# Running sums of the log gates: made once per 512 columns and loaded per chunk, with the chunks' factor differences on GpSimd

## The chip, the cores and the metric

One core of one Trainium2 chip runs the whole step in one launch. Its engines are TensorE (PE, with its weight loads PEld), VectorE (DVE), ScalarE (ACT), GpSimd (POOL) and SyncE (SP), which issues every DMA. The metric is the device time of one execution in microseconds (us), lower is better.

## The reference, cut to what matters

One layer of a hybrid encoder is computed for 2064 prompt rows (16 meta rows and 2048 new ones) and for 8 sample streams of 16 rows. Two mixers run on the same input: gated linear attention (GLA) and sparse attention over selected keys. The change concerns the gates of the first:

```python
log_f = log_sigmoid(g_low @ gla_w2 + gla_gate_b) / 16        # [t, 4 heads, 128]
# per block of tokens, heads apart:
b = cumsum(log_f, axis=tokens)
a[i, j] = sum_d q[i,d] k[j,d] exp(b[i,d] - b[j,d])   for j <= i
o = (q * exp(b)) @ S + a @ v
S = exp(b_end)[:, None] * S + (k * exp(b_end - b)).T @ v
```

## The kernel before, in words

Phase 1 makes all projections in three groups of columns and writes them to HBM (`d_...`). Phase 2 runs the sparse attention for the query blocks 15 down to 8, then blocks 7 to 0 together with the GLA projection, then the merge and the output projection.

*The attention* of a block makes, per head, logits in PSUM (lines 1110 and 1111, tile `pl`, 3 buffers). DVE reads each piece out of PSUM, adds the mask and takes the maximum (line 1112: `lgl`, `lgu`, `mx`). ACT takes the exponential (line 1117), PE transposes the probabilities (line 1046, `px`), ACT or DVE copies them out (1054, 1056), and PE multiplies with the values (1070, `oo`).

*The side work* is a generator (`side_work`, line 1214) that the attention advances as it goes: `gla_gates`, the samples' attention (`attend_sample`), the samples' GLA (`gla_sample`), the meta rows (`gla_meta`), then 16 chunks of 128 tokens (`gla_chunk`). Its first 13 steps are given a priority 1500 ahead, so that they run beside the last projections of phase 1.

*The gates* (`gla_gates`, line 652) go through the 2192 columns in 5 slices of up to 512, each in two groups of two heads: four `[128, 512]` products on PE (line 666, `pg`, 2 buffers), absolute value on ACT (667), minimum on DVE (668, `gx`), exponential and logarithm on ACT, subtraction on POOL (675), and a store of the log gates to `d_lf` (676). The tiles `gx` and `ge` of `[128, 2, 512]` share three buffers.

*A chunk* loads its 128 columns of log gates (683, `x`), and DVE makes the running sums with one scan per head (687, `b`, restarted by the zero in `rst`). `gla_factors` (693) then takes differences of those sums: 12 tensor-tensor instructions on DVE for a chunk and 6 for the samples, into `f`; ACT takes the exponential of `f` (715) and of `x` (859). `gla_pairs` and three `gla_level`s scale q and k with these factors on POOL (`q`, `m`, `mq`), PE multiplies them (735, 756), and DVE puts the blocks into the matrix `a` with masked copies (737, 738, 761). The next chunk's `b` may be written when the exponential of the last sum (864, `end`) has read this chunk's.

The order of each engine's instructions is fixed when the program is built: a scheduler plays the program through on a timeline of its own and writes down, engine by engine, what it would start first, with priorities given by the place in the source. An engine then works through its list strictly in order, so one instruction that waits holds up all behind it. A changed duration or dependency moves rows on every engine from that point on.

Of the kernel before, what the change touches and what calls it, by code (L numbers as in the profile page):

```python
# [10 lines left out]
F32 = mybir.dt.float32  # L11
# [6 lines left out]
OP = mybir.AluOpType  # L18
# [3 lines left out]
P = 128  # L22
DM = 1024
KT = 8
META = 16
# [51 lines left out]
TT = META + NT * P  # L77
# [8 lines left out]
def nkeys(j):  # L86
    return META + P * (j + 1)
# [31 lines left out]
class Trunk:  # L119
# [73 lines left out]
    def scratch(self, ctx):  # L193
        dr = ctx.enter_context(self.tc.tile_pool(name="dr", bufs=1, space=DRAM))
        d = {}
        for n, s, t in (
            ("gq", [512, TT], F32), ("gk", [512, TT], F32), ("gl", [16, TT], F32), ("lf", [512, TT], F32),
            ("gv", [TT, 1024], F32), ("gr", [TT, 1024], F32),
            ("q", [2048, TT], F32R),
            ("ih", [512, TT], F32R), ("il", [512, TT], F32R),  # L200
            ("kd", [P, 4, TT], F32R), ("v", [TT, 256], F32), ("z", [TT, 1024], F32),
            ("ma", [1024, TT], F32), ("mb", [1024, TT], F32),
            ("oa", [1024, TT], F32), ("ob", [1024, TT], F32), ("ya", [1024, TT], F32), ("h", [TT, 1024], F32),
        ):
            d[n] = dr.tile(s, t, name="d_" + n)
        d["mask"] = {j: dr.tile([P, nkeys(j)], BF16, name=f"d_mask{j}") for j in range(16)}
        d["mask"]["s"] = dr.tile([P, SKEY], BF16, name="d_masks")
        d["xt"] = [dr.tile([P, KT, n], F32, name=f"d_xt{q}") for q, n in enumerate(PCN)]
        self.d = d
# [441 lines left out]

    def gla_gates(self):

        nc = self.nc
        for c in range(0, TT, 512):
            n = min(512, TT - c)
            gl = self.gt.tile([16, 512], F32, name="gl", tag="x")
            nc.sync.dma_start(gl[:, :n], self.d["gl"][:, c : c + n])
            xs, es = [], []
            for g in range(2):  # L660
                x = self.sb.tile([P, 2, 512], F32, name="gx", tag="s4", bufs=SKB)
                e = self.sb.tile([P, 2, 512], F32, name="ge", tag="s4", bufs=SKB)
                for u in range(2):
                    h = 2 * g + u
                    ps = self.pg.tile([P, 512], F32, name="pg")
                    nc.tensor.matmul(ps[:, :n], self.w2[:, h * P : (h + 1) * P], gl[:, :n], start=True, stop=True)
                    self.act(e[:, u, :n], ps[:, :n], AF.Abs, bias=self.gb[:, h : h + 1])
                    self.ts(x[:, u, :n], ps[:, :n], self.gb[:, h : h + 1], OP.add, 0.0, OP.min)
                self.act(e[:, :, :n], e[:, :, :n], AF.Exp, scale=-1.0)
                xs.append(x)  # L670
                es.append(e)
            for g in range(2):
                x, e = xs[g][:, :, :n], es[g][:, :, :n]
                self.act(e, e, AF.Ln, bias=1.0)
                self.tt(x, x, e, OP.subtract, eng=nc.gpsimd)
                nc.sync.dma_start(self.d["lf"][2 * g * P : (2 * g + 2) * P, c : c + n].rearrange("(h p) t -> p h t", p=P), x)
            yield

    def gla_decay(self, c, r):

        nc = self.nc
        x = self.gt.tile([P, 4, P], F32, name="x")
        nc.sync.dma_start(x[:, :, :r], self.d["lf"][:, c : c + r].rearrange("(h p) t -> p h t", p=P))
        b = self.gt.tile([P, 4, P + 1], F32, name="b")
        nc.gpsimd.memset(b[:, :, 0:1], 0.0)
        for h in range(4):
            nc.vector.tensor_tensor_scan(b[:, h, 1 : 1 + r], self.rst[:, h, :r], x[:, h, :r], 0.0, OP.mult, OP.add)
        return x, b

    def gla_eng(self, kind):  # L690
# [2 lines left out]
    def gla_factors(self, b, levels):  # L693


        e = self.nc.vector
        f = self.gt.tile([P, 924], F32, name="f")
        out, at = [], 0
        for r, s in levels:
            n = P // (r * s)  # L700
            first = b[:, :, :P].rearrange("p h (n c s) -> p h n c s", c=r, s=s)[:, :, :, :, 0]
            last = b[:, :, 1:].rearrange("p h (n c s) -> p h n c s", c=r, s=s)[:, :, :, :, s - 1]
            group = lambda t, w: t.to_broadcast([P, 4, n, w])
            def put(w, x, y):
                nonlocal at
                t = f[:, at : at + 4 * n * w]
                at += 4 * n * w
                self.tt(t.rearrange("p (h n c) -> p h n c", h=4, n=n), x, y, OP.subtract, eng=e)
                return t.rearrange("p (m c) -> p m c", c=w)
            fs = [put(r, first, group(first[:, :, :, 0:1], r)), put(r, group(last[:, :, :, r - 1 : r], r), last)]  # L710
            if r == 4:
                fs.append(put(2, first[:, :, :, 2:4], group(last[:, :, :, 0:1], 2)))
                fs.append(put(1, first[:, :, :, 3:4], last[:, :, :, 1:2]))
            out.append(fs)
        self.act(f[:, :at], f[:, :at], AF.Exp, scale=1.0 / 16)
        return out
# [754 lines left out]
```

## Time and profile before

| | before |
|---|---|
| median of 3 runs | 3657.09 us (3652.93 to 3662.06) |
| the profiled execution, its own time | 3653.39 us |
| its span, first to last instruction | 3651.6 us |
| busy: PE, DVE, ACT, POOL | 96%, 70%, 40%, 29% |
| mean granted clock of TensorE | 0.985 |

The profile is of one execution. Busy times overlap from engine to engine, and a PE that is shown busy may still be waiting inside a pipelined instruction. In the span the gates' stage lies at 1677 to 1745 us, phase 1's last projection ends at about 1858 us, the samples' GLA runs from about 1914 us, and the 16 chunks from about 2010 to 2690 us.

### The profile page before, as it was taken

The numbers are of one execution on the slowest core, as the hardware profiler recorded it, in microseconds if no ns is written. First come the engines' busy times: TensorE is split into PE (matmuls) and PEld (weight loads), VectorE is DVE, ScalarE is ACT, GpSimd is POOL, SyncE is SP. The second block draws the span as 40 slices with busy tenths as digits, with TensorE's granted clock in tenths as the row PEclk, the third lists the DMA queues.
The fourth block names the chain that finished last, engine by engine and source line by source line (L and its number), as shares of the span: only waits on it lengthen the run. The fifth ranks groups of instructions, "written<-read, shape, count | busy, mean of one in ns | idle before, by whom it ended". The sixth has DMA issues, their size and how long they took to land.

```text
span 3651.6 us, 65899 instructions
## 1 busy us (share of the span) xinstructions
PE 3516.6 (96%) x24196; PEld 3224.6 (88%) x24196; DVE 2568.0 (70%) x5971; ACT 1451.5 (40%) x3084; POOL 1048.6 (29%) x1220
## 2 busy tenths in 40 slices
PE   7999999999999999999989999999999999989999
PEld 7999999999999999998976778777778888879998
DVE  7748997799999988943246877777765666555444
ACT  4444223433334234325434555555665443431110
POOL 3122343242343344344301433334410000012221
PEclk9999999999999999999999999999999999999999
DMA  8642443263442345363653333233343345564432
GB/s 266 196 127 84 136 124 96 84 180 106 122 127 75 117 136 166 115 173 122 160 170 106 84 92 85 80 92 85 85 116 89 94 106 138 150 193 140 121 114 62
DMA packets 535810, 448.78 MB, mean 123 GB/s; under 512 B 94032, under 2 KB 507856, under 8 KB 535488
## 3 DMA queue, kind: packets, MB, share of 16 engines
q1 hardware_dynamic: 535488, 444.58, 42.4%
q8 instruction: 190, 3.11, 0.4%
q14 instruction: 132, 1.08, 0.1%
HBM read 288.01 MB, written 156.44 MB: 122 GB/s over the span
## 4 chain that ended last, share of the span: by engine, by line
PE 75%; DVE 13%; DMA 5%; ACT 2%; issue 2%; POOL 1%; SPq 1%; POOLq 0%; DVEq 0%; ACTq 0%
PE pp L266 12%; PE pp L264 12%; PE pp L265 12%; PE oo L1070 6%; PE px L1046 4%; PE pd L264 3%; PE pd L266 3%; PE pd L265 3%; PE pl L1110 2%; PE pl L1111 2%; PE fo L264 2%; PE fo L265 2%; PE fo L266 2%; DVE junk L149 1%; DVE sc L152 1%
## 5 line engine op out<-in xcount | busy, mean ns | idle before, releaser
L149 DVE TENSOR_SCALAR_CACHE_REDUCE junk<-sc,cand 128x272 bf16<-128x272 f32 (+6 forms) x512 | 701.7, 1371 | 17.0
L143 POOL TENSOR_TENSOR wlo<-raw,whi 128x512 fp32r<-128x512 f32 x360 | 487.9, 1376 | 768.0 <-ACT whi L158 704.3
L266 PE MATMUL pp<-whi,xl 128*128 128x256 f32 (+3 forms) x1952 | 560.4, 288 | 4.4 <-DVE xl L143 4.4
L264 PE MATMUL pp<-whi,xh 128*128 128x256 f32 (+3 forms) x1952 | 561.7, 288 | 3.1 <-ACT whi L158 2.1
L264 PE MATMUL pp<-xh,whi 128*128 128x384 f32 (+2 forms) x1728 | 563.0, 326 | 1.4 <-ACT whi L158 1.4
L265 PE MATMUL pp<-xl,whi 128*128 128x384 f32 (+2 forms) x1728 | 563.2, 326 | 0.0
L266 PE MATMUL pp<-xh,wlo 128*128 128x384 f32 (+2 forms) x1728 | 562.1, 326 | 0.1
L265 PE MATMUL pp<-wlo,xh 128*128 128x256 f32 (+3 forms) x1952 | 560.9, 288 | 0.0
L266 PEld LDWEIGHTS pp<-whi,xl 128*128 128x128 f32 (+1 forms) x1952 | 370.4, 190 | 14.6 <-DVE xl L143 6.9
L264 PEld LDWEIGHTS pp<-whi,xh 128*128 128x128 f32 (+1 forms) x1952 | 371.4, 190 | 11.2 <-issue 3.0
L265 PEld LDWEIGHTS pp<-wlo,xh 128*128 128x128 f32 (+1 forms) x1952 | 371.4, 190 | 5.4 <-issue 2.3
L1112 DVE CUSTOM_DVE_ANT_0 lgl<-pl,mkl 128x348 f32<-128x348 f32 (+8 forms) x608 | 297.3, 510 | 83.6 <-PE pl L1111 48.0
L1110 PE MATMUL pl<-kd,q 128*128 128x348 f32 (+14 forms) x800 | 308.1, 388 | 32.7 <-DVE mx L1112 23.9
L264 PE MATMUL pd<-xh,wh 128*128 128x242 f32 (+3 forms) x1152 | 327.9, 285 | 8.6 <-ACT wh L1328 3.8
L264 PEld LDWEIGHTS pp<-xh,whi 128*128 128x128 f32 x1728 | 324.4, 188 | 2.7 <-ACT whi L158 2.0
L266 PE MATMUL pd<-xh,wl 128*128 128x242 f32 (+3 forms) x1152 | 324.6, 282 | 0.8 <-POOL wl L143 0.8
L265 PE MATMUL pd<-xl,wh 128*128 128x242 f32 (+3 forms) x1152 | 325.1, 282 | 0.3 <-DVE xl L143 0.3
L266 PEld LDWEIGHTS pp<-xh,wlo 128*128 128x128 f32 x1728 | 324.1, 188 | 1.2 <-POOL wlo L143 0.4
L265 PEld LDWEIGHTS pp<-xl,whi 128*128 128x128 f32 x1728 | 324.4, 188 | 0.7
L158 ACT CAST whi<-raw 128x512 fp32r<-128x512 f32 (+1 forms) x344 | 199.1, 622 | 314.8 <-DMA raw<-in_w_in 201.3
L155 ACT ACTIVATE lgl<-lgl,mx 128x1040 f32<-128x1040 f32 (+7 forms) x256 | 249.8, 976 | 181.5 <-DVE mx L1114 177.6
L1118 POOL COPY pmeta<-lgl 128x48 f32<-128x48 f32 x256 | 58.7, 229 | 771.4 <-ACT lgl L155 765.0
(250 smaller groups left out, 7842.7 us busy)
## 6 DMA issues: line engine op xcount, KB each, us to landing
raw<-in_w_in SPq DMA_DIRECT2D x360, 256.0 KB, 3.2
q<-d_q SPq DMA_DIRECT2D x272, 128.0 KB, 3.0
d_h<-x SPq DMA_DIRECT2D x17, 512.0 KB, 3.4
d_gv<-en SPq DMA_DIRECT2D x68, 128.0 KB, 2.1
d_gr<-en SPq DMA_DIRECT2D x68, 128.0 KB, 1.8
d_z<-en SPq DMA_DIRECT2D x68, 128.0 KB, 1.7
gr<-d_gr SPq DMA_DIRECT2D x17, 512.0 KB, 3.6
v<-d_gv SPq DMA_DIRECT2D x17, 512.0 KB, 3.9
```

Source lines behind the costliest of these rows:

```text
L143: (eng or self.nc.vector).tensor_tensor(out, a, b, op=op)
L149: (eng or self.nc.vector).tensor_scalar(out, a, s1, s2, op0=op0, op1=op1, **kw)
L155: self.nc.scalar.activation(out, a, f, **kw)
L158: (self.nc.vector.tensor_copy if self.spare else self.nc.scalar.copy)(out, src)
L264: mm(ps, ah(k), bh(k), start=k == 0, stop=False)
L265: mm(ps, ah(k), bl(k), start=False, stop=False)
L266: mm(ps, al(k), bh(k), start=False, stop=k == n - 1)
L1046: nc.tensor.transpose(ps[:, 2 * s + u, :], pe[u][a // KLOW][:, a % KLOW : a % KLOW + P], self.ident[:])
L1070: self.nc.tensor.matmul(oo[0][64 * o : 64 * o + 64, k : k + 2, :], self.v[:, s0 + s, d : d + 64], t[:, 2 * s : 2 * s + 2], start=self.fres ...
L1110: nc.tensor.matmul(ps[:, :m], q[:, u, :], kd, start=True, stop=False)
L1111: nc.tensor.matmul(ps[:, :m], q[:, 2 + u, :], kd, start=False, stop=True)
L1112: nc.vector.tensor_tensor_reduce(lg[z1][:, a : a + m], ps[:, :m], mk[z1][:, a : a + m], 1.0, NEG, OP.add, OP.max, mx[:, s : s + 1])
```

## The change

- A new scratch array `d_ls` holds running sums. After the subtraction, the gates' stage runs the scan over its whole slice on DVE, two heads of `[128, 400]`, `[128, 512]` or `[128, 256]` per group, into the tile `ge`, and stores it to `d_ls` beside `d_lf`. `rst` is read flat, so the sums restart every 128 columns.
- The slices are cut at chunk boundaries: 400 columns (the 16 meta columns are scanned apart), three times 512, and 256. There are still five.
- A chunk loads its sums into `b` by a second DMA in place of four scans.
- The differences in `gla_factors` go to POOL; the loop, the instructions and their shapes are the same.

```diff
     def gla_gates(self):
-        for c in range(0, TT, 512):
-            n = min(512, TT - c)
+        rst = self.rst[:].rearrange("p c t -> p (c t)")
+        cuts = [0, *range(META + 3 * P, TT, 512), TT]
+        for c, end in zip(cuts, cuts[1:]):
+            n = end - c
...
                 self.act(e, e, AF.Ln, bias=1.0)
                 self.tt(x, x, e, OP.subtract, eng=nc.gpsimd)
-                nc.sync.dma_start(self.d["lf"][2 * g * P : (2 * g + 2) * P, c : c + n].rearrange("(h p) t -> p h t", p=P), x)
+                for a, b in ((0, META), (META, n)) if not c else ((0, n),):
+                    for u in range(2):
+                        nc.vector.tensor_tensor_scan(e[:, u, a:b], rst[:, : b - a], x[:, u, a:b], 0.0, OP.mult, OP.add)
+                for name, t in ("lf", x), ("ls", e):
+                    nc.sync.dma_start(self.d[name][2 * g * P : (2 * g + 2) * P, c : c + n].rearrange("(h p) t -> p h t", p=P), t)
             yield
     def gla_decay(self, c, r):
         x = self.gt.tile([P, 4, P], F32, name="x")
-        nc.sync.dma_start(x[:, :, :r], self.d["lf"][:, c : c + r].rearrange("(h p) t -> p h t", p=P))
         b = self.gt.tile([P, 4, P + 1], F32, name="b")
         nc.gpsimd.memset(b[:, :, 0:1], 0.0)
-        for h in range(4):
-            nc.vector.tensor_tensor_scan(b[:, h, 1 : 1 + r], self.rst[:, h, :r], x[:, h, :r], 0.0, OP.mult, OP.add)
+        for t, src in (x[:, :, :r], "lf"), (b[:, :, 1 : 1 + r], "ls"):
+            nc.sync.dma_start(t, self.d[src][:, c : c + r].rearrange("(h p) t -> p h t", p=P))
         return x, b
     def gla_factors(self, b, levels):
-        e = self.nc.vector
+        e = self.nc.gpsimd
```

Three places show what that does to the order. Line numbers behind the change are six higher (L761 becomes L767, L1112 becomes L1118). First DVE in the middle of the chunks, before: the attention's reads of PSUM are `lgl` and `lgu`, the scans of the next chunk are `b<-rst,x`, printed there as a scalar-tensor-tensor form.

```order
L761 COPY_PREDICATED a<-lm,pg 128x32x6
L687 SCALAR_TENSOR_TENSOR b<-rst,x 128x128 x4
L1112 ISA lgl,mx<-pl,mkl 128x348
L1112 ISA mx 128x1
L1112 ISA lgl,mx<-pl,mkl 128x344
L1112 ISA mx 128x1
L983 RECIPROCAL rs<-sums 128x8
L761 COPY_PREDICATED a<-lm,pg 128x32x6
```

At the like place, the masked copies of a chunk's last level, the changed program has on DVE:

```order
L767 COPY_PREDICATED a<-lm,pg 128x32x6
L1120 TENSOR_REDUCE mx<-mx 128x1
L767 COPY_PREDICATED a<-lm,pg 128x32x6
L767 COPY_PREDICATED a<-lm,pg 128x32x4
L1118 ISA lgl,mx<-pl,mkl 128x348
L1118 ISA mx 128x1
L767 COPY_PREDICATED a<-lm,pg 128x32x4
L1062 COPY st_25770<-px 128x512
```

The four scans ahead of the attention's reads are gone, and so are the runs of 12 differences `f<-b` that stood some 20 rows further on. Those runs now stand on POOL, between a chunk's last products and the next chunk's first; on that engine the changed program has:

```order
L143 TENSOR_TENSOR m<-m,f 128x512
L143 TENSOR_TENSOR mq<-mq,f 128x512
L143 TENSOR_TENSOR f<-b 128x256 x2
L143 TENSOR_TENSOR f<-b 128x128
L143 TENSOR_TENSOR f<-b 128x64 x3
L143 TENSOR_TENSOR f<-b 128x32
L143 TENSOR_TENSOR f<-b 128x16 x3
L143 TENSOR_TENSOR f<-b 128x8
L143 TENSOR_TENSOR f<-b 128x4
L143 TENSOR_TENSOR m<-k,x 128x256
L143 TENSOR_TENSOR mq<-q,x 128x64x4 x2
```

POOL works through one chunk after the other, and the differences are queued in that one line. In the gates' stage DVE of the changed program has the new scans (line 681, `ge<-rst,gx`) among the minima `gx`, the copies of projections `en` and the casts of weights `whi`:

```order
L149 TENSOR_SCALAR gx<-pg,gb 128x512 x2
L158 CAST whi<-raw 128x512 x2
L158 COPY en<-pp 16x256
L158 CAST whi<-raw 128x512
L681 SCALAR_TENSOR_TENSOR ge<-rst,gx 128x512 x2
L158 COPY en<-pp 128x256
L149 TENSOR_SCALAR gx<-pg,gb 128x512 x2
L158 COPY en<-pp 128x256
L681 SCALAR_TENSOR_TENSOR ge<-rst,gx 128x512 x2
L149 TENSOR_SCALAR gx<-pg,gb 128x512 x2
```

Each pair of scans stands ahead of the next group's minima.

## Rows read from the trace of the kernel before

**Rows 1.** The page, part 1: busy time, share of span, instructions per engine.
```profile
PE 3516.6 (96%) x24196; PEld 3224.6 (88%) x24196; DVE 2568.0 (70%) x5971; ACT 1451.5 (40%) x3084; POOL 1048.6 (29%) x1220
```

**Rows 2.** Stages: window, length, each engine busy (instructions), granted clock, DMA share, GB/s.
```profile
2038.00:2639.00 601.00, 565.38 (x3835) 466.67 (x3834) 455.30 (x1632) 338.12 (x724) 231.53 (x364) 0.98 0.31 85
2640.00:2690.00 50.00, 49.24 (x346) 40.72 (x346) 34.17 (x129) 29.57 (x75) 12.40 (x23) 1.00 0.26 69
1677.00:1745.00 68.00, 68.00 (x440) 51.65 (x439) 26.33 (x46) 59.64 (x67) 36.20 (x22) 1.00 0.44 138
1850.00:1900.00 50.00, 39.62 (x196) 31.96 (x196) 25.16 (x91) 20.60 (x45) 1.37 (x5) 0.83 0.68 192
```

**Rows 3.** The same view: 14 stretches of 8 us around the scans.
```profile
2195.00:2203.00 8.00, 6.15 (x32) 5.62 (x31) 7.39 (x25) 4.35 (x8) 3.57 (x7) 0.81 0.48 151
...
2322.00:2330.00 8.00, 5.17 (x27) 4.56 (x26) 7.56 (x27) 4.95 (x10) 4.76 (x7) 0.79 0.28 78
...
sum 112.00, PE 97.31 PEld 79.67 DVE 95.72 ACT 68.14 POOL 60.89; mean PE 6.95 PEld 5.69 DVE 6.84 ACT 4.87 POOL 4.35
```

**Rows 4.** The same view: 15 stretches of 8 us around the differences.
```profile
2163.00:2171.00 8.00, 4.96 (x29) 3.87 (x29) 7.25 (x29) 4.61 (x9) 5.07 (x7) 0.89 0.22 53
...
sum 120.00, PE 103.60 PEld 83.40 DVE 108.62 ACT 66.30 POOL 66.81; mean PE 6.91 PEld 5.56 DVE 7.24 ACT 4.42 POOL 4.45
```

**Rows 5.** Order of time, 2322 to 2328 us: start, length, operation [idle before].
```profile
2322.33 0.50 DVE L1112 CUSTOM_DVE_ANT_0 lgl<-pl,mkl 128x348 f32<-128x348 f32 x1
...
2322.76 3.14 DVE L687 TENSOR_TENSOR_SCAN b<-rst,x 128x128 f32<-128x128 f32 x4
...
2323.23 0.31 PE L1111 MATMUL pl<-kd,q 128*128 128x320 f32 x1
...
2325.82 0.48 DVE L1112 CUSTOM_DVE_ANT_0 lgl<-pl,mkl 128x344 f32<-128x344 f32 x1
...
2326.36 0.66 PE L1110 MATMUL pl<-kd,q 128*128 128x348 f32 x1 [2.83 <-DVE mx L1112]
```

**Rows 6.** Waits, 2038 to 2640 us: total us, times, longest us.
```profile
PEld pl L1110 <- DVE mx L1112: 28.2, 30, 3.1
...
PE pl L1110 <- DVE mx L1112: 20.8, 14, 2.8
...
POOL mq L143 <- ACT f L155: 16.1, 9, 2.7
```

**Rows 7.** Groups of instructions, whole span: count, busy us, mean ns, idle before.
```profile
L756 PE MATMUL pg<-mq,m 128*128 128x192 f32 (+1 forms) x400 | 81.9, 331 | 0.9 <-POOL pmeta L1118 0.5 <-DVE mx L1114 0.2 <-DVE state L152 0.2
...
L143 DVE TENSOR_TENSOR f<-b 128x128 f32<-128x128 f32 (+4 forms) x198 | 55.5, 348 | 2.0 <-POOL mq L143 1.9
...
L687 DVE TENSOR_TENSOR_SCAN b<-rst,x 128x128 f32<-128x128 f32 (+1 forms) x72 | 40.0, 615 | 2.3 <-DMA x<-d_lf 2.3
...
L666 PE MATMUL pg<-gl,w 16*128 16x512 f32 (+1 forms) x40 | 19.4, 573 | 0.0
```

**Rows 8.** Line 687, the scans: shortest, median and longest in ns.
```profile
L687 DVE TENSOR_TENSOR_SCAN b<-rst,x x72: 162/410/1317, 1914.3 to 2616.4; 128x128 f32<-128x128 f32 x68, 128x16 f32<-128x16 f32 x4
```

**Rows 9.** Groups by shape on POOL, 1900 to 2700 us.
```profile
L143 POOL TENSOR_TENSOR mq<-mq,f 128x256 f32<-128x256 f32 x49 | 32.5, 664 | 17.9 <-ACT f L155 17.3
...
L1118 POOL COPY pmeta<-lgl 128x48 f32<-128x48 f32 x102 | 24.0, 235 | 248.5 <-ACT lgl L155 242.1 <-DMA q<-d_q 5.5 <-PE pl L1111 0.7
...
L143 POOL TENSOR_TENSOR mq<-mq,f 128x128 f32<-128x128 f32 x49 | 21.4, 436 | 0.0
L143 POOL TENSOR_TENSOR m<-k,x 128x256 f32<-128x256 f32 x17 | 15.6, 920 | 29.5 <-issue 28.1 <-POOL mq L143 1.4
```

**Rows 10.** Tile gx: shortest, median, longest ns; first and last start; landing.
```profile
L149 DVE TENSOR_SCALAR gx<-pg,gb x20: 357/742/754, 1679.9 to 1740.0; 128x512 f32<-128x512 f32 x16, 128x144 f32<-128x144 f32 x4
...
DMA to landing us min/median/max: 1.9/2.8/3.5
```

**Rows 11.** SP's own waits: total us, times, longest us.
```profile
SPq L683 <- POOL mq L143: 73.4, 14, 12.5
```

More of the change, by code (lines that the diff above doesn't have):

```diff
@@ L196, in scratch @@
         for n, s, t in (
-            ("gq", [512, TT], F32), ("gk", [512, TT], F32), ("gl", [16, TT], F32), ("lf", [512, TT], F32),
+            ("gq", [512, TT], F32), ("gk", [512, TT], F32), ("gl", [16, TT], F32), ("lf", [512, TT], F32), ("ls", [512, TT], F32),
             ("gv", [TT, 1024], F32), ("gr", [TT, 1024], F32),
```

## The prediction

> **What bounds the kernel now.** I read the busy shares first: PE 3516.6 us of a 3651.6 us span, 96% [rows 1]. Work taken from DVE or given to POOL therefore counts only where PE waits for it. The table of stages says where that is. In the chunks' stage, 2038 to 2639 us, PE is busy 565.38 of 601 us, so it idles 35.6 us, with a granted clock of 0.98; right behind the last differences, 2640 to 2690 us, it idles 0.8 of 50 us at 1.00; in the gates' stage, 1677 to 1745 us, it idles not at all [rows 2].
>
> Next I cut the chunks' stage where the changed instructions stand. Fourteen stretches of 8 us around the chunks' scans hold 112 − 97.31 = 14.7 us of PE idle [rows 3], fifteen around the differences 120 − 103.60 = 16.4 us [rows 4]. Together that is 31.1 of the stage's 35.6 us in 232 of its 601 us. The other 369 us have 4.5 us, 1.2%. DVE is busy 95.72 + 108.62 = 204.3 of 232 us there, 88%, and (455.3 − 204.3) / 369 = 68% elsewhere.
>
> One stretch in order of time shows the mechanism. DVE reads a piece of logits, then runs four scans for 3.14 us; the next read starts at 2325.82; PE, which needs the PSUM buffer, stands until 2326.36 and has idled 2.83 us, put down to DVE's maximum [rows 5]. The list of waits agrees: PE and its weight loads wait for that line 20.8 and 28.2 us in this stage (the two overlap and are not added), 2.8 and 3.1 us at the longest [rows 6]. The clock follows: three of the stretches shown have 0.81, 0.79 and 0.89 granted, which means that part of each ran at the lower of the two levels, 1.2 GHz [rows 3, 4].
>
> **Term 1, the bursts leave DVE.** 68 scans of 128 columns and 4 of 16 go (40.0 us with what they are held up), and 198 differences (55.5 us) [rows 7]. Fifteen chunks' differences and fourteen chunks' scans lie in the stretches above, about 55.5 × 15 / 17 + 40.0 × 14 / 18 = 80 us of the 204.3. What is left there is 124 of 232 us, 53%, less than the 68% at which PE lost 1.2%. At that rate the stretches would still idle 2.8 us, so at most 31.1 − 2.8 = 28.3 us of idle can go. The clock costs (1 − 0.98) × 601 = 12 us, 9 to 15 with the rounding; I count half, 6 us, since part of it runs while PE stands idle anyway. The ceiling is 28.3 + 6 = 34 us, or 43 if nothing of the clock's loss overlaps. I take three quarters of 34, 26 us: DVE keeps the masked copies and state updates of the same chunk, and the list is scheduled anew, so some waits will reappear at other rows. The floor is nothing gained, if the waits only move. The samples' and the meta rows' bursts before 2038 us I count at nothing; they come on top if anything.
>
> **Term 2, the differences on POOL.** Per chunk: two of 256 elements, one of 128, three of 64, one of 32, three of 16, one of 8 and one of 4. POOL takes 664 to 920 ns for 256, 436 for 128, and 235 ns for a copy of 48 [rows 9]. With 0.84, 0.44 and, for the nine small ones, 0.28 between the last two, that is 1.7 + 0.4 + 2.5 = 4.6 us a chunk and about 75 us in all; 50 us if all are as quick as that copy, 100 us if the small ones take what 128 does. POOL is busy 231.5 of 601 us, 39%, so it ends near 50% [rows 2]. What hides it is the attention: PE lost 0.9 us in all in front of the 400 products that POOL feeds [rows 7]. The cost is nothing as long as a chunk's chain has that slack; what it costs without it is the slower rival below.
>
> The trace shows that DVE's scans pay for POOL's company: 410 ns at the median and 1317 at the longest for the same instruction [rows 8]. The Trainium skill, "SBUF — State Buffer" (Who interferes with whom), says that a DVE instruction with two SBUF inputs and a GpSimd one that reads SBUF exclude each other for a whole instruction; "Perfetto Trace Analysis" (Optimizing Scalar/DVE Operations) warns that moving work between the two might therefore not help. Here it speaks less against the move than it seems: the scans and differences are the two-input instructions, and both leave this stage's DVE, while the reads of PSUM run at 0.48 to 0.50 us right beside POOL's work [rows 5]. By the warning term 1 would be nothing, which is the second case below.
>
> **Term 3, the gates' stage.** Added on DVE are 24 scans: twelve of 512 columns, four each of 384, 256 and 16. From 162 ns (16 columns) to 410 (128) is 2.2 ns a column [rows 8], so 1.26, 0.98 and 0.69 us for the long ones, 22 us in all. Held up by POOL each adds up to 1317 − 410 = 0.9 us, 44 us in all. DVE is busy 26.3 of 68 us there, ACT 59.6 [rows 2]: ACT sets the pace, 60.1 us for nine steps of a group, 6.7 us each [rows 10]. A pair of scans is 2.5 to 4.3 us and stands ahead of the next group's minima (0.74 us each), which free the PSUM buffers for line 666. That line waits for nothing now [rows 7], and the changed list puts more projection rows between its products. I take 3 us: that a pair of scans delays a weight cast or a minimum once or twice. Bounds: nothing, if ACT stays the slower; 12 us, if all scans slow down in proportion (1317 / 410 = 3.2, so 4.0 us each and 8 us a pair, 1.3 us over a step of 6.7 us, nine times).
>
> **Term 4, DMAs and the change of phase.** Ten stores and 18 loads are added on SP. A chunk's `b` must wait for the previous chunk's last exponential; behind that wait on SP stand loads of q for the attention. SP already waits 73.4 us for the slot of `x`, once 12.5 us [rows 11], in a stage where PE idles 35.6 us in all, so the loads of q bear waits of that kind. The gates' longer chain also pushes the samples' work later, from beside the last projections into the change of phase, where PE idles 10.4 of 50 us at 0.83 [rows 2]. It can fill that hole or lengthen the chain behind it: −4 to +6 us, taken as +1.
>
> **Sum.** −26 + 0 + 3 + 1 = −22 us against the profiled execution's 3653.39, 3631. The median of the runs lies 3.7 us above that execution, so 3635 us.
>
> **Rivals.**
> - The waits only move (no change, 3655 us). DVE's bursts go, but the masked copies, POOL's later products and the new order take their place, and term 1 returns a quarter or less: −6 + 4 = −2 us. For it: every list from the gates on is new, and DVE stays about 60% busy. Against it: 87% of the idle lies in 39% of the stage, exactly at these instructions.
> - POOL becomes the chunk's bound (slower, 3670 us). POOL does one chunk after another, and the differences now stand between the last product of one and the first product of the next, where DVE made them beside POOL's work. POOL already waits 16.1 us for the exponential of these factors [rows 6], so they are on the chunk's chain. It decides once a chunk's first product comes later than PE's list has it by more than the slack: then PE stands, in order, with the attention behind it. Fully exposed that is 15 × 4.6 = 69 us; half exposed, as I take it, 35 us, and with −26 of term 1 and +4 of terms 3 and 4 that is +13 us on 3657. Against it: 0.9 us lost there now, and POOL half idle.
> - The whole ceiling comes (3618 us): −43 + 4 = −39 us from 3657.
>
> **Chances.** Forecast (3635) 0.50, ceiling 0.12, no change 0.23, POOL 0.15. What a measurement of this kernel can tell from no change is 0.3%, 11 us, so faster means under 3646. The forecast falls short of that in a few cases of its own, which the no-change case gives back in part: faster 0.61, same 0.24, slower 0.15. The range takes in the ceiling and reaches to where the POOL case begins: 3608 to 3668 us; the forecast's own is 3622 to 3646.
>
> **What would show it.** In the changed profile the chunks' stage should hold about 12 us of PE idle in place of 35.6, with a clock of 0.99 or more; PE's waits at the logits for DVE's maximum should fall to half; DVE's total should fall by some 60 us and POOL's rise by 50 to 100. Term 2 is wrong if PE's idle in front of the level products (now 0.9 us) grows to several us or POOL's differences average over 0.6 us; term 3 if PE idles in the gates' stage; term 4 if the hole at the change of phase grows. The forecast as a whole fails if the chunks' stage is not shorter.

## The result: 3602 us, faster, by more than the range allowed

| | before | changed |
|---|---|---|
| median | 3657.32 us (3652.93 to 3662.06, 4 runs) | 3602.16 us (3595.52 to 3604.86, 4 runs) |
| span of the profiled execution | 3651.6 us | 3598.6 us |
| mean granted clock | 0.985 | 0.99 |

The ratio is 0.9846, with a 95% interval of 0.9827 to 0.9865. The direction was forecast, the size was not: 22 us were forecast, 55 came, and the range ended at 3608 us.

The page's part 1 of the changed kernel, to be read against [rows 1]:

```profile
PE 3487.7 (97%) x24196; PEld 3215.9 (89%) x24196; DVE 2512.2 (70%) x5725; ACT 1450.1 (40%) x3084; POOL 1107.5 (31%) x1418
```

DVE lost 56 us and 246 instructions, POOL gained 59 us and 198. PE has the same number of matmuls as before and is still busy 29 us less. The stages, as in [rows 2] (the chunks' stage, the stretch behind it, the gates' stage, the change of phase, each where it now lies):

```profile
2060.00:2637.00 577.00, 568.62 (x3997) 481.23 (x3994) 404.00 (x1458) 346.98 (x760) 289.69 (x561) 1.00 0.36 99
2637.00:2690.00 53.00, 44.92 (x309) 34.26 (x308) 32.52 (x114) 36.56 (x80) 10.35 (x17) 0.94 0.54 151
1682.00:1762.00 80.00, 78.00 (x493) 61.34 (x494) 47.95 (x69) 59.42 (x66) 38.19 (x22) 0.96 0.52 173
1860.00:1910.00 50.00, 43.67 (x255) 35.70 (x255) 32.10 (x118) 26.48 (x57) 1.40 (x6) 0.90 0.78 214
```

In the chunks' stage PE idles 8.4 us in place of 35.6, at a clock of 1.00 in place of 0.98. But look at the matmuls: 3997 in 577 us, 142.3 ns of busy time each, where before there were 3835 in 601 us, 147.4 ns each. For 3835 matmuls the stage now needs 554 us, 47 less. Idle is 27.5 us of that, and 20 us come out of time that was shown as busy. The mix of matmuls differs between the two windows, so this split is rough.

To compare equal work I cut the trace at matmuls: from the first product of the attention's logits (line 1110, now 1116) to its 576th, the last of blocks 15 to 8. The same table for that stretch, of the kernel before:

```profile
1870.00:2803.00 933.00, 877.34 (x5883) 710.17 (x5883) 672.72 (x2381) 516.38 (x1103) 289.23 (x471) 0.97 0.34 93
```

and of the changed one:

```profile
1874.50:2754.40 879.90, 853.97 (x5911) 706.07 (x5911) 598.55 (x2130) 516.93 (x1110) 342.53 (x668) 0.99 0.38 106
```

Nearly the whole gain lies here: 53 us, of which 30 are idle (55.7 to 25.9 us) and 23 busy time. The clock is a large part of the second: by the trace's records of it 50 us of the stretch were at the lower level before and 16.5 are now. At half speed that is 25 and 8 us of clock not granted, 17 us less. The stretch begins 4.7 us later than before (1869.8 to 1874.5), and what follows it is 4.7 us shorter (848.9 to 844.2).

The waits at the logits over 680 us (2010 to 2690; total, times, longest), of the kernel before:

```profile
PEld pl L1110 <- DVE mx L1112: 29.8, 34, 3.1
...
PE pl L1110 <- DVE mx L1112: 21.2, 16, 2.8
```

and of the changed one:

```profile
PEld pl L1116 <- DVE mx L1118: 5.0, 13, 1.0
...
PE pl L1116 <- DVE mx L1118: 1.6, 4, 0.7
```

Waits of 3 us are gone; what is left is at most 1.0 us. One chunk's start in order of time, which answers to [rows 5]:

```profile
2242.22 3.67 POOL L143 TENSOR_TENSOR f<-b 128x256 f32<-128x256 f32 x12
...
2242.55 0.51 DVE L1118 CUSTOM_DVE_ANT_0 lgl<-pl,mkl 128x344 f32<-128x344 f32 x1
...
2243.24 0.42 PE L1116 MATMUL pl<-kd,q 128*128 128x384 f32 x1
2243.25 0.55 DVE L1118 CUSTOM_DVE_ANT_0 lgu<-pl,mku 128x384 f32<-128x384 f32 x1
...
2243.92 0.55 DVE L1118 CUSTOM_DVE_ANT_0 lgu<-pl,mku 128x384 f32<-128x384 f32 x1
2244.19 0.46 PE L1116 MATMUL pl<-kd,q 128*128 128x348 f32 x1
```

POOL makes all twelve differences in 3.67 us while DVE reads logits at 0.51 to 0.55 us a piece, and no product of PE shows an idle time ahead of it.

Groups of instructions, whole span, to be read against [rows 7 and 10]:

```profile
L762 PE MATMUL pg<-mq,m 128*128 128x192 f32 (+1 forms) x400 | 80.6, 329 | 2.4 <-POOL mq L143 2.2
...
L143 POOL TENSOR_TENSOR f<-b 128x128 f32<-128x128 f32 (+4 forms) x198 | 61.8, 353 | 5.7 <-DMA b<-d_ls 4.7
...
L681 DVE TENSOR_TENSOR_SCAN ge<-rst,gx 128x512 f32<-128x512 f32 (+3 forms) x24 | 28.0, 1214 | 18.7 <-POOL gx L143 18.7
...
L669 PE MATMUL pg<-gl,w 16*128 16x512 f32 (+2 forms) x40 | 19.7, 576 | 1.5 <-DVE gx L149 1.5
```

The differences cost POOL 61.8 us, 353 ns each, and 4.7 us of waiting for the loaded sums. PE waits 2.2 us in all for POOL's products. The gates' scans take 28.0 us. SP's wait for the slot of `x` fell from 73.4 us [rows 11] to 42.7:

```profile
SPq L693 <- POOL mq L143: 42.7, 13, 8.8
```

### The profile page after: what moved, and what is told of

Its sections match the earlier page's. It is cut to its first block, busy times and chain, and to the rows that moved or that the text cites. A ratio compares the mean times of both kernels' runs of the same rounds, so it can differ in the third digit from the quotient of the medians.

```text
span 3598.6 us, 65922 instructions
## 1 busy us (share of the span) xinstructions
PE 3487.7 (97%) x24196; PEld 3215.9 (89%) x24196; DVE 2512.2 (70%) x5725; ACT 1450.1 (40%) x3084; POOL 1107.5 (31%) x1418
## 5 line engine op out<-in xcount | busy, mean ns | idle before, releaser
L1118 DVE CUSTOM_DVE_ANT_0 lgl<-pl,mkl 128x348 f32<-128x348 f32 (+8 forms) x608 | 296.4, 511 | 103.3 <-PE pl L1117 65.2
L152 DVE SCALAR_TENSOR_TENSOR sc<-rl,iw,sc 128x388 f32<-128x388 f32 (+16 forms) x308 | 216.9, 743 | 71.4 <-ACT rl L155 70.0
```

The costliest lines, as they stand in the source:

```text
L152: self.nc.vector.scalar_tensor_tensor(out, a, s, b, op0=op0, op1=op1)
L1118: nc.vector.tensor_tensor_reduce(lg[z1][:, a : a + m], ps[:, :m], mk[z1][:, a : a + m], 1.0, NEG, OP.add, OP.max, mx[:, s : s + 1])
```

## Experiments

Theory A is the prediction's mechanism: the chunks' scans and differences hold up DVE's reads of logits, and what leaves DVE comes back as time of PE. Rivals: what got shorter is the chunk's own chain of work, whose sums are now loaded ahead, and DVE's time as such does not matter (B); the two parts relieve DVE only together (C); and, after the first four runs, O: a good part of the gain is only another order of the rows, which any change of a duration brings. Each run was timed beside the kernel before, whose medians were 3652 to 3656 us in these sets; a ratio is to that, with its 95% interval.

**The parts alone.** Sums made with the gates and loaded, differences left on DVE (diff against the changed kernel):

```diff
-        e = self.nc.gpsimd
+        e = self.nc.vector
```

> Scans in the gates' stage and loaded by chunks, differences left on DVE. Theory A (what DVE has in its list beside the attention's reads costs, each burst for itself): the scans' stretches held a bit under half of PE's idle and more than half of the low clock, less some 5 us in the gates' stage: about 25 us faster than before, 3632 us (3622 to 3642). Rival B (the chunk's chain is what got shorter, since its sums are loaded ahead and nothing on DVE precedes them; DVE's time as such does not matter): nearly the whole gain, 3600 to 3612 us. Rival C (the two parts relieve DVE only together, below some load): at most 10 us faster, 3647 to 3657 us.

Measured: 3616.63 us, 0.9903 (0.9874 to 0.9932).

Only the differences moved (gates' stage, stores and chunk scans as before, `e = self.nc.gpsimd`):

> Differences on GpSimd, scans left where they were. A: about 30 us faster than before, 3627 us (3617 to 3637), so that with the scans' part the 55 us are made up. B: no gain, 3650 to 3660 us, since the chain keeps its scans and gets slower differences. C: at most 10 us faster, 3647 to 3657 us.

Measured: 3632.78 us, 0.9946 (0.993 to 0.9961). Each part has a gain alone, 36 and 20 us, which add up to the 55, where B expected none of the differences and C at most 10 us of either. The sums gave more than A allows them (3622 us at the least). Taken by themselves these two runs do not part A from O, since the next ones show that another order alone is worth 20 us.

The gates' stage as changed, with sums made and stored that nobody loads; the chunks work as before (diff against the changed kernel):

```diff
-        for t, src in (x[:, :, :r], "lf"), (b[:, :, 1 : 1 + r], "ls"):
-            nc.sync.dma_start(t, self.d[src][:, c : c + r].rearrange("(h p) t -> p h t", p=P))
+        nc.sync.dma_start(x[:, :, :r], self.d["lf"][:, c : c + r].rearrange("(h p) t -> p h t", p=P))
+        for h in range(4):
+            nc.vector.tensor_tensor_scan(b[:, h, 1 : 1 + r], self.rst[:, h, :r], x[:, h, :r], 0.0, OP.mult, OP.add)
...
-        e = self.nc.gpsimd
+        e = self.nc.vector
```

> The gates' stage makes and stores the sums as in the changed kernel, but nobody loads them: a chunk makes its own with scans, and the differences stay on DVE. It prices what is added in the gates' stage alone. A and C: 3 to 9 us slower than before, 3660 to 3666 us, at the end of phase 1. B: the same price. Another reading, that the new order of the rows alone brought the gain: faster than before by 10 us or more.

Measured: 3632.38 us, 0.994 (0.9919 to 0.9962). This kernel only adds work, takes nothing from the chunks, and is 20 us faster. A, B and C had it 3 to 9 us slower; the other reading named there, that the new order alone brings a gain, is the one that came. No cost of an instruction explains it, and it is where theory O comes from.

Four unread scans in each chunk of the changed kernel, first form:

```diff
+        w = self.gt.tile([P, 4, P], F32, name="w")
+        for h in range(4):
+            nc.vector.tensor_tensor_scan(w[:, h, :r], self.rst[:, h, :r], x[:, h, :r], 0.0, OP.mult, OP.add)
```

> The changed kernel, and each chunk also runs four scans of its log gates on DVE into a tile that nobody reads, so DVE has the scans' time back while no chain depends on them. A: it loses what the scans' part gained, 25 to 30 us, and comes to 3625 to 3635 us. B: within 5 us of the changed kernel, 3597 to 3607 us. C: most of the gain goes, 3640 us or more.

Measured: 3680.7 us, 1.0075 (1.0051 to 1.0099). It is not the test that was meant: all but 4 of the gates' 40 products came after the last projection of phase 1 (1813 us), the last of them at 1906 us in place of 1756. The new tile lies in the chunks' pool, and I take it that it moved other tiles, which the trace does not show. The run says nothing of the scans.

**The order alone.** One number of the scheduler's priorities, no work added or removed, first in the kernel before and then in the changed one:

```diff
-EARLY = 1500
+EARLY = 1400
```

> The kernel before with one number of the planner changed (EARLY 1500 to 1400): no work is added or removed on any engine; from the last projection of phase 1 on the rows come in another order, and the samples' part ends later among the attention's work, as it does in the changed kernel. Theory A (the gain of the changed kernel is VectorE's relief from the chunks' bursts): 3645 to 3662 us, no change. Theory O (about 20 us of the 55 are the order of the rows, as the run that only made the sums in the gates' stage suggests): 3625 to 3642 us, and fewer stretches of the attention at a clock below 1.00. Any value outside 3620 to 3665 says that the order alone moves more than either theory gives it.

Measured: 3625.01 us, 0.9925 (0.991 to 0.994): 29 us faster with the same instructions. Its waits at the logits over the same 680 us:

```profile
PEld pl L1110 <- DVE mx L1112: 21.4, 30, 3.5
PE pl L1110 <- DVE mx L1112: 14.0, 12, 3.1
```

They are about as long as before, one by one, but there are fewer. The time is in O's range; A had expected no change.

> The changed kernel with the same number changed (EARLY 1500 to 1400), the work on every engine as in the changed kernel. Theory A: 3595 to 3610 us, as the changed kernel. Theory O: the order's share may be lost or not, 3595 to 3625 us; above 3615 it would say that a good part of the gain hangs on one order of the rows.

Measured: 3609.81 us, 0.9884 (0.9869 to 0.9899), which both theories allow.

The kernel before with the new cuts of the gates' slices alone:

```diff
-        for c in range(0, TT, 512):
-            n = min(512, TT - c)
+        cuts = [0, *range(META + 3 * P, TT, 512), TT]
+        for c, end in zip(cuts, cuts[1:]):
+            n = end - c
```

> The kernel before with the changed kernel's cuts of the gates' stage alone (400, 512, 512, 512 and 112 columns at the end in place of 512 steps from 0); scans and differences stay in the chunks on VectorE. Theory A: no change, 3645 to 3662 us. Theory O: as the run that only made the sums, 3625 to 3640 us, since that run differs from before in the cuts, the sums and the order that follows from them. If it is as slow as before, the cuts are not what gave that run its 20 us.

Measured: 3633.72 us, 0.9948 (0.9933 to 0.9963), as fast as with the unread sums, and again in O's range and not in A's. (The last slice has 256 columns, not the 112 that the expectation names.) So the sums themselves cost the gates' stage nothing that shows: the first product of the logits starts at 1874.3 us with the cuts alone, at 1874.5 in the changed kernel.

Two more orders of the kernel before (EARLY 1450 and 1600) and one of the changed kernel (1600):

> The kernel before with EARLY 1450, no work added or removed: a third order of the rows; the chunks' part lies between those of 1500 (the kernel before) and 1400. Reading U (the order of the kernel before is an unlucky one, by some 20 us): 3620 to 3640 us. Reading L (the order at 1400 is a lucky one): 3645 to 3660 us.

> The kernel before with EARLY 1600: a fourth order, in which the samples' part and the chunks begin earlier among the attention's work than in any of the others. Reading U: 3620 to 3642 us. Reading L: 3645 to 3665 us. If the place of the side work among the attention is what counts (later is better), this is the slowest of all, 3655 to 3675 us.

> The changed kernel with EARLY 1600: work on every engine as in the changed kernel, but samples and chunks begin as early among the attention's work as in the kernel before. If the relief of VectorE is worth 25 to 32 us whatever the order, and that place costs 20: 3615 to 3630 us. If the place costs only where VectorE has the bursts (order and relief are one and the same gain): 3598 to 3610 us. Above 3635 the change would have no gain of its own in this order.

Measured: 3642.34 us, 0.9965 (0.9953 to 0.9977); 3649.56 us, 0.998 (0.9968 to 0.9991); 3605.56 us, 0.9861 (0.9844 to 0.9877). Neither "unlucky" nor "lucky" is the whole story, and the changed kernel at 1600 came out where relief and order are one gain (3598 to 3610), not where the relief is worth 25 to 32 us whatever the order (3615 to 3630). By EARLY:

| | 1400 | 1450 | 1500 | 1600 | cuts only |
|---|---|---|---|---|---|
| before | 3625.0 | 3642.3 | 3657.3 | 3649.6 | 3633.7 |
| changed | 3609.8 | | 3602.2 | 3605.6 | |

The same work takes 32 us more or less in the kernel before, and 8 in the changed one. Every order of the changed kernel is faster than every order of the kernel before; the gain is 15, 55 or 44 us at equal EARLY. The kernel before stands at the slow end of its orders, the changed kernel at the fast end of its own. Place does not decide it: 1600 brings the side work earliest and is slow with the bursts, not without them. Nor do the waits at the logits rank the orders: at 1600 they are 14.2 us on PEld and 7.3 on PE, less than the 21.4 and 14.0 at 1400, in a kernel that takes 25 us longer. What makes one order of the kernel before slower than another stays open.

Some of these kernels can be compared with less of the order in it. In seven of them the stretch from the logits' first product to the 576th holds the very same 5912 matmuls, by what they write and read, and in the first two of these in the very same order. In the mean a matmul of the other six stands 6 to 20 places from where it stands in the changed kernel's stretch. Their lengths (the last three kernels come in the next part):

| | stretch, us | PE idle | DVE busy |
|---|---|---|---|
| before, EARLY 1400 | 911.5 | 44.7 | 666.1 |
| sums made, unread (the gates' stage as changed) | 911.2 | 46.6 | 667.5 |
| sums made and loaded, differences on DVE | 897.2 | 36.1 | 635.1 |
| changed: differences on POOL too | 879.9 | 25.9 | 598.6 |
| changed, four unread scans in a row | 904.5 | 43.4 | 629.7 |
| changed, unread scans spread, first form | 910.0 | 43.2 | 625.3 |
| changed, unread scans spread, second form | 890.2 | 32.0 | 630.9 |

With the gates' stage kept as changed, loading the sums shortens the stretch by 14 us and moving the differences by another 17; the whole times, 3632, 3617 and 3602 us, fall by 16 and 14. The second step leaves the chunk's chain its links and only takes the differences off DVE (353 ns each on POOL, 348 on DVE before), so B does not explain it. The orders still differ a little from step to step, and the changed kernel's orders by EARLY differ by 8 us.

**The load put back.** Four unread scans per chunk again, in a pool of their own, meant to move no other tile; PE's order stays close to the changed kernel's:

```diff
+        if r == P and self.spares:
+            w = self.spares.tile([P, 4, P], F32, name="w")
+            for h in range(4):
+                nc.vector.tensor_tensor_scan(w[:, h, :r], self.rst[:, h, :r], x[:, h, :r], 0.0, OP.mult, OP.add)
...
+            self.spares = inner.enter_context(tc.tile_pool(name="spares", bufs=1, side="right"))
```

> The changed kernel with four scans on VectorE in every 128-row chunk whose result nobody reads, in a pool of its own so that the other tiles stay where they are; the order of TensorE's rows is the changed kernel's for the phases up to the last sixth. It adds 64 scans or so of about 0.6 us, 35 to 40 us on VectorE, as the chunks of the kernel before had them. Theory A: what the scans cost in place comes back, 16 us as the step from the sums alone to sums loaded by the chunks gave: 3612 to 3625 us, and the clock dips behind the bursts return. Theory O: the order is kept, so no more than 5 us: 3598 to 3607 us.

Measured: 3621.89 us, 0.9915 (0.9898 to 0.9931), 20 us slower than the changed kernel, as A has it and O has not. The long waits are back; in order of time PE's idle stands right behind the scans, though these took only 1.36 us here. The dips of the clock that were expected hardly came back: by the trace's records of the clock 10 of these 680 us are at the lower level, where the kernel before has 31 and the changed one 7. Waits over the 680 us:

```profile
PEld pl L1120 <- DVE mx L1122: 16.0, 25, 4.2
PE pl L1120 <- DVE mx L1122: 9.7, 10, 3.8
```

Order of time:

```profile
2311.14 2.34 DVE L149 TENSOR_SCALAR ss<-ss 128x2 f32<-128x2 f32 x1 [0.78 <-ACT sq L155]
...
2312.93 1.36 DVE L697 TENSOR_TENSOR_SCAN w<-rst,x 128x128 f32<-128x128 f32 x4
2314.21 0.48 DVE L1122 CUSTOM_DVE_ANT_0 lgl<-pl,mkl 128x344 f32<-128x344 f32 x1
...
2314.76 0.43 PE L1120 MATMUL pl<-kd,q 128*128 128x348 f32 x1 [1.55 <-DVE mx L1122]
```

The scans are not the only thing that came back. Here DVE's own `ss`, a small instruction that took 2.34 us, stands ahead of them. Over the whole run DVE stood idle for 27.9 us in front of these scans, until the load of `x` had landed, with the reads of logits behind them in its list:

```profile
L697 DVE TENSOR_TENSOR_SCAN w<-rst,x 128x128 f32<-128x128 f32 x68 | 31.3, 521 | 28.0 <-DMA x<-d_lf 27.9
```

In the kernel before, the scans waited 2.3 us for that load in all [rows 7], and its long waits stand behind scans and differences that ran one behind the other. So this run puts back two things, the scans and a wait of DVE for a load, and does not say how much of the 20 us is whose.

Is it the burst or the load on DVE? Nearly the same number of scans (64, in place of 68 with the samples' four), one after the first pass and one after each level, each in a tile of its own:

```diff
+    def gla_spare(self, b, h):
+        w = self.spares.tile([P, P], F32, name="w", tag=f"w{h}")
+        self.nc.vector.tensor_tensor_scan(w[:], self.rst[:, h, :], b[:, h, 1:], 0.0, OP.mult, OP.add)
...
+        self.gla_spare(b, 0)
...
+            self.gla_spare(b, 1 + level)
```

> The changed kernel with the same number of unread scans on VectorE as the run with four in a row at each chunk's start (j4), but one after the chunk's first pass and one after each of its three levels; the order of TensorE's rows differs little. If it is the burst that costs (four scans together hold up the row's maxima): 3603 to 3612 us, less than half of j4's 20 us. If it is VectorE's load, wherever it stands: 3616 to 3626 us, as j4.

Measured: 3625.25 us, 0.9919 (0.9891 to 0.9948). Taken as it stands, this is the reading "load, wherever it stands". But in the trace 32 of the 64 scans still stood four in a row and only 3 singly, since nothing tied them to their places, and DVE waited 18.7 us in front of them for the loaded sums. So a second form, which reads what DVE has just masked (`a[:, h, :]` in place of `b[:, h, 1:]`) and in which all 64 stand singly:

> As the run with the spread scans (m1), in which 32 of the 64 unread scans still came four in a row, but each reads the chunk's products that VectorE has just masked, so that all 64 stand singly between other instructions: the same load on VectorE, no burst. If it is the burst that costs: 3603 to 3610 us. If it is the load, wherever it stands: 3616 to 3628 us. Between the two, some of each.

Measured: 3610.41 us, 0.9875 (0.9855 to 0.9895), 8 us above the changed kernel, though these scans took more of DVE than the bursts did, 43.7 us against 31.3. Waits at the logits:

```profile
PEld pl L1122 <- DVE mx L1124: 8.9, 20, 1.0
...
PE pl L1122 <- DVE mx L1124: 3.4, 8, 0.7
```

No wait is over 1.0 us, as in the changed kernel. So DVE's load as such costs little: some 8 us of the 20, and the order of the rows differs a little between these runs, which was worth 8 us in the changed kernel. The table of equal matmuls says the same: with DVE busy 631, 630 and 625 us in the three runs with unread scans the stretch takes 890, 904 and 910. What the single scans lost is the burst, but also the wait for a load: these read what DVE itself has just written, and DVE idled 0.7 us in front of them in all. Which of the two makes the other 12 us was not parted; that would take four scans in a row that wait for no load.

**POOL's slack, and what is left.** Every difference issued twice on POOL:

```diff
-                self.tt(t.rearrange("p (h n c) -> p h n c", h=4, n=n), x, y, OP.subtract, eng=e)
+                for _ in range(2):
+                    self.tt(t.rearrange("p (h n c) -> p h n c", h=4, n=n), x, y, OP.subtract, eng=e)
```

> The changed kernel in which POOL makes each of a chunk's differences twice, into the same tile: some 66 us more on POOL in all, about 4 us in each 128-row chunk. Rival of the prediction (POOL becomes the chunk's bound): each chunk ends 2 to 4 us later and matmuls wait for it, 3620 to 3660 us. My reading (POOL has slack in the chunk, and the planner's rows leave room for it): 3598 to 3610 us, POOL's busy time up by 60 to 70 us and no long wait of a matmul for POOL.

Measured: 3613.76 us, 0.9887 (0.9867 to 0.9906), 11.6 us above the changed kernel: above my reading, below the rival's. The groups:

```profile
L143 POOL TENSOR_TENSOR f<-b 128x16 f32<-128x16 f32 (+6 forms) x396 | 123.9, 354 | 7.7 <-DMA b<-d_ls 7.0
...
L763 PE MATMUL pg<-mq,m 128*128 128x192 f32 (+1 forms) x400 | 80.4, 328 | 1.5 <-DVE a L768 1.4
```

62 us more on POOL, and PE does not wait for it in front of the level products. The stretch of the attention is as long as in the changed kernel (882 and 880 us) but holds 5787 matmuls in place of 5911. The chunks end later, their last level product at 2674.6 us in place of 2618.3, and 120 products of `pd`, a projection that starts behind the chunks, come only after the stretch, which 11 us more follow than in the changed kernel. POOL is not the bound, but its slack is not endless either, as far as 11.6 us can show it where orders differ by 8.

Three of four copies from PSUM on ACT in place of two of three:

```diff
-TURNS = "DAA", "DDA"
+TURNS = "DAAA", "DDA"
```

> The changed kernel with the turns of the attention's stretch set to DAAA in place of DAA (of every four copies from PSUM three go to ACT and one to VectorE, in place of two of three), which takes some more load off VectorE. If what is left of the stalls still comes from VectorE: 3590 to 3600 us. If the burst work was all that VectorE cost TensorE: 3598 to 3610 us, no gain, since ACT's copies take longer.

Measured: 3598.79 us (3592.72 to 3603.06), 0.985 (0.9825 to 0.9875), the lowest median of all. The difference from the changed kernel, 3 us, is smaller than the spread of either's runs, so it shows no gain from further relief, nor excludes a small one. The reason that the expectation gives against a gain does not hold: a copy of `[128, 512]` out of PSUM takes 583 ns on ACT and 685 on DVE here.

## Why the prediction was wrong, step by step

- *What bounds the kernel, and where:* right. The chunks' stage was shortened, and the waits at the logits for DVE's maximum went (29.8 to 5.0 us; half was forecast). Unread scans in a row, behind a load, brought them back, single ones did not.
- *Term 1 (bursts leave DVE, 26 us):* this is the step that failed, in its size. Equal rows of the chunks' stage (80th to 448th product of the logits) went from 619.4 to 576.2 us, 43 us, with some 40 matmuls more between them, and the stretch ahead of them, with the samples' GLA, gave 9.5 us more, which I had counted at nothing. Of the 43 us 30 are idle and 13 busy time, and by the records of the clock 30.7 us of these rows were at the lower level before, which is 15.4 us of clock not granted, and none of them now. So the ceiling itself held: 28.3 us of idle with the clock's 15 is the 43 that the prediction names and did not take. Three choices were too small. I took three quarters of the ceiling. I counted the clock's loss half, 6 us, though idle shows only what stands between matmuls, not those that run long at the lower clock. And "some waits will reappear at other rows" has no fixed sign: the new order was worth something itself, and that it carried this pair to the upper ceiling is in part luck. The kernel before took 617 to 621 us for these rows in four orders and 597 in the two runs (EARLY 1400, unread sums) that share a fifth; the changed kernel took 576, 584 and 594 (3913 to 4017 matmuls between them, so these are not quite equal work). Between the averages lie about 30 us, not far from the 26. For the whole time the five of before in the table average 3642 us and the three of the changed kernel 3606: 36 us apart. The other 19 of the 55 are the two kernels' places among their own orders. With so few orders these averages are rough.
- *Term 2 (differences on POOL, free):* 61.8 us in all against 75 forecast, 3.67 us in the chunk shown against 4.6, mean 353 ns. The idle in front of the level products grew from 0.9 to 2.4 us. As said, nearly nothing, though the doubled run, with 62 us more, took 11.6 us longer.
- *The warning weighed there:* the Trainium skill, "Perfetto Trace Analysis" (Optimizing Scalar/DVE Operations), says that the two share an SBUF read port, which a two-port DVE instruction holds as an exclusive lock, so that moving work between them might not help. Here it helped, as far as one order of each kernel can show: with the sums loaded, moving the differences took the kernel from 0.9903 (0.9874 to 0.9932) to 0.9846 (0.9827 to 0.9865), and the same 5912 matmuls from 897 to 880 us. DVE's reads of PSUM ran at 0.51 to 0.55 us beside POOL's differences. The 0.9946 of the differences moved alone does not show it by itself, since new cuts alone gave 0.9948.
- *Term 3 (+3 us; scans of 22 us, 44 at most):* the scans took 28.0 us; PE idles 2.0 of 80 us there; the first product of the logits comes 4.7 us later, and as late without any sums, so this is not the scans' cost. The +3 did not come.
- *Term 4 (+1 us):* the hole at the change of phase went from 10.4 to 6.3 us of idle at 0.90 in place of 0.83, and SP's wait for `x` from 73.4 to 42.7 us. Small, as forecast; the rows behind the attention's stretch are 4.7 us shorter, which makes up for its later start.
- *The rivals:* "the waits only move" and "POOL becomes the bound" came in none of the three orders of the changed kernel. "The whole ceiling comes" (3618) was the nearest: its 43 us came, but it leaves out the 9.5 us ahead of the chunks and takes off 4 us for terms 3 and 4 that did not come.

## What to carry to other kernels

Idle time alone is no ceiling where the granted clock falls as well: add what the clock withholds, in full, price the same work in the stages ahead, and afterwards compare the length of equal rows. Here 43 us came where 26 were taken, and 9.5 where nothing was counted. Where a scheduler writes each engine's list, a single kernel is one draw from its orders: here the same work varied by 32 us, more than the 22 that were forecast for the edit, so time both kernels in several orders before a gain is put down to the edit. Short work in front of another engine's releases cost less in single pieces than in a row, though here the single pieces also no longer stood behind a load. At the same three values of EARLY the kernel before varied by 32 us and the changed one by 8; whether the relief is why, three orders of each do not show.

## What was not expected of the hardware

A scan of `[128, 128]` by itself takes some 0.4 us (384 to 426 ns in the 21 of 64 that met no instruction of POOL), but one that meets POOL's products can be held for several of them; the other 43 have a median of 670 ns. Line 698 of the run with single scans (shortest, median, longest in ns):

```profile
L698 DVE TENSOR_TENSOR_SCAN w<-rst,a x64: 384/466/3477, 2050.2 to 2628.6; 128x128 f32<-128x128 f32 x64
```

One of them in order of time:

```profile
2327.05 0.74 POOL L143 TENSOR_TENSOR mq<-q,x 128x256 f32<-128x256 f32 x1
...
2327.70 2.53 DVE L698 TENSOR_TENSOR_SCAN w<-rst,a 128x128 f32<-128x128 f32 x1
2327.76 1.16 POOL L143 TENSOR_TENSOR m<-m,f 128x512 f32<-128x512 f32 x1
2328.88 1.06 POOL L143 TENSOR_TENSOR mq<-mq,f 128x256 f32<-128x256 f32 x2
2329.89 0.35 POOL L1130 COPY pmeta<-lgl 128x48 f32<-128x48 f32 x1
2330.15 0.48 DVE L1124 CUSTOM_DVE_ANT_0 lgl<-pl,mkl 128x344 f32<-128x344 f32 x1
```

The scan begins while one product of POOL is ending, just ahead of three others, and ends when these and the copy behind them end; the read of PSUM that follows takes its usual 0.48 us. The Trainium skill, "SBUF — State Buffer" (Who interferes with whom), has such a DVE instruction with two SBUF inputs and a GpSimd one that reads SBUF contend for a shared read interface, and calls the shared pair an exclusive lock. The trace agrees, and adds that the wait need not end with one instruction of POOL. A scan's price thus depends on what POOL does beside it. That this is one reason why equal work differs so much from order to order is a guess; no run tests it.
